# The first attention group's loads move into the last conv slot of the first pass, and the two query places change roles

## The chip, the cores and the metric

The kernel runs on one core of one Trainium2 chip, as one program. The metric is the device time of a run in microseconds (us). Five engines work side by side, each through its own list of instructions in order: TensorE (PE; its weight loads are PEld), VectorE (DVE), ScalarE (ACT), GpSimd (POOL) and SyncE (SP). SP computes nothing here: it issues nearly all DMAs, and its own waits are shown under the name SPq.

## The reference, cut to what matters

One layer of a hybrid encoder runs over 2048 prompt frames and 32 frames of a running stream, with 1024 channels. The input projection gives eight parts of 512 columns; four feed a conv branch and four an attention branch.

```python
xn = rmsnorm(x, norm_in)
h, bg, cg, zc, q, k, v, za = project_in(xn, w_in)        # xn @ w_in, split
yc = bg * short_conv(cg * h, conv_w, S) * jax.nn.silu(zc)
ya = band_attention(qc, k_band, v_band, rel, valid, rel_bias) * jax.nn.silu(za)
x = x + merge_out(yc, ya, norm_conv, norm_att, w_out)    # rmsnorm of each, then @ w_out
x = per_layer_embed(x, p, ple_norm, w_ple_gate, w_ple_proj)
y = rmsnorm(x, final_norm)
```

The band attention has 8 heads of 64 channels. A chunk of 64 frames attends to itself and to the 8 chunks before it. The 32 frames of the running stream attend to 512 cached keys and to themselves. Besides y, the newest keys, values and conv rows are returned.

## The kernel before

**Precision.** Every operand of a product is kept as a high and a low part in fp32r, and each product is three matmuls (high by high, high by low, low by high).

**On-chip memory.** One tile `GR` of 43,008 columns holds all matmul operands, at offsets written by hand. In the first part it holds the transposed input in five chunks of frames (`CHUNKS`; `Xh`, `Xl`) at columns 0 to 33,280. Chunk 0 (256 frames) lies at 0 to 4,096 and chunk 1 (384 frames) at 4,096 to 10,240. Two weight places `WS` follow, and from 41,472 (`O_SP`) 1,536 spare columns. Attention reuses the columns of chunks 0 and 1: keys `K` at 0 and 1,536, values `V` at 3,072, two places for transposed probabilities at 6,144 and 7,680, and the first of two query places at 9,216; the second query place and the two gate places `Z` lie in the spare columns.

**Stages.** (1) Projections of k, q, v and the attention gate, slot by slot; the results go to DRAM as `kd`, `qs`, `vd` and `zd`. (2) The conv branch: 8 slots `u`, each with two blocks of 128 weight columns, in `conv()`. The slots are passed three times: pass one over chunks 0 and 1 (`u` = 0 to 7), pass two over chunks 2 and 3 (8 to 15), pass three over chunk 4 (16 to 23). Pass one also stores the split weights in DRAM (`store_wc`, line 1054), and passes two and three read them back, 2 MB for a slot (`load_wc`, line 1060). (3) Beside passes two and three runs attention: `dense()` yields after every three conv matmuls, and the loop at the end hands out pieces of the generator `attention()` by the share of conv work done, from 3% (`FIRST`) on. (4) The output projection and the embedding, tile by tile.

**One conv slot.** For each chunk and block, 24 matmuls (line 1085) fill one PSUM bank. A slot of kind "B" then multiplies into `T2` (line 1102, DVE), applies the gate (line 1105 ACT, 1106 DVE), multiplies again (line 1107, POOL) and stores `T2` to `yd` (line 1108, SP). There is one `T2`: the next chunk's line 1102 needs that store to have landed. `conv()` yields 16 times for a chunk, the last time after the chunk's store.

**Attention.** There are 36 groups (4 head pairs by 9 spans of frames), and a step for each head. `load_kq(g)` loads a group's keys (line 447) and queries (line 454) for two heads in six DMAs of 128 KB; `load_vz(g)` loads its values (line 463, 256 KB) and gate (line 467, 128 KB). Queries of group g lie in `Q[g % 2]`. `emit_s(n, a)` (line 546) multiplies queries by keys on PE for one half of step n's frames; maximum, exponential, scaling, transposes (lines 618, 628) and the product with the values (lines 662, 664) follow.

**Order of SP.** SP issues in program order, and what it waits for holds up all behind it. At the end of pass one it issues, in this order: at `u` = 6 the weights of slot 8, four loads of the score bias (lines 474, 482) and the store of slot 7's weights (line 1054); in slot 7 the two stores of `T2`; then slot 9's weights; then the loads of attention groups 0 and 1. POOL masks the bias (lines 491, 492) before it comes to slot 7's line 1107.

```python
O_Q = [9216, O_SP]
    for u in range(8):
        s = NP1 + u
        store_wc(s)
        for i, _ in enumerate(conv(u, psm)):
            if i == KT:
                split_w(s + 1)
                load_w(s + 2)
        if u >= 6:
            load_wc(u + 2)
```

The functions that the change touches follow.

Of the kernel before, what the change touches and what calls it, by code (L numbers as in the profile page):

```python
# [26 lines left out]
KT = 8  # L27
# [12 lines left out]
O_SP = O_WS[1] + 4096  # L40
# [5 lines left out]
O_K = [0, 1536]  # L46
O_V = 3072
O_PT = [6144, 7680]
O_Q = [9216, O_SP]
O_Z = [O_SP + 1024, O_SP + 1280]  # L50

O_WO = XO[2]
# [11 lines left out]
def hybrid_encoder_kernel(  # L64
# [43 lines left out]
    def R(off, *shape):  # L108
        n = 1
        for s in shape:  # L110
            n *= s
        v = GR[:, off:off + n]
        return v if len(shape) == 1 else v.rearrange("p (a b) -> p a b", a=shape[0])
# [52 lines left out]
    def cols(kind, i):  # L166
        return DC * "hBCzqkva".index(kind) + 128 * i
# [8 lines left out]
    def load_w(s):  # L176
        if s >= NS:
            return
        (k0, i0), (k1, i1) = slots[s]
        if k0 == k1:  # L180
            c = cols(k0, i0)
            sp.dma_start(RAW, win[:, c:c + 256].rearrange("(k p) n -> p k n", p=128))
        else:
            for j, (kk, ii) in enumerate(slots[s]):
                c = cols(kk, ii)
                sp.dma_start(RAW[:, :, j * 128:(j + 1) * 128],
                             win[:, c:c + 128].rearrange("(k p) n -> p k n", p=128))

    def split_w(s, ks_=range(KT)):
        if s >= NS:  # L190
            return
        wh, wl = WS[s % 2]
        for k in ks_:
            act.activation(wh[:, k], RAW[:, k], AF.Copy, scale=cT[:, k:k + 1])  # L194
            dve.scalar_tensor_tensor(wl[:, k], RAW[:, k], cT[:, k:k + 1],  # L195
                                     wh[:, k].bitcast(F32), ALU.mult, ALU.subtract)
# [225 lines left out]
    K = [R(o, RING * 128) for o in O_K]  # L422
    Q = [[[R(o + 512 * h + 256 * b, 256) for b in range(2)] for h in range(2)] for o in O_Q]
    V = R(O_V, RING, 256)
# [13 lines left out]
    def load_kq(g):  # L438

        if g >= len(groups):  # L440
            return
        p, m = groups[g]
        t0, kn, qn = (256 * m, 256, 256) if m < 8 else (T, KW + S, S)
        k0 = t0 % (RING * 128)
        for h in range(2):
            rows = slice((2 * p + h) * HD, (2 * p + h + 1) * HD)
            sp.dma_start(K[h][:, k0:k0 + kn].bitcast(F32),
                         kd[:, rows, t0:t0 + kn].rearrange("b c t -> c b t"))
            for b in range(2):
                q = Q[g % 2][h][b]  # L450
                if m == 8:
                    pool.memset(q[:, 0:2 * S].bitcast(F32), 0.0)
                    q = q[:, h * S:(h + 1) * S]
                sp.dma_start(q[:, 0:qn].bitcast(F32),
                             qs[b, rows, t0:t0 + qn].unsqueeze(1).to_broadcast([HD, 2, qn]))

    def load_vz(g):
        if g >= len(groups):
            return
        p, m = groups[g]  # L460
        m0, m1 = (2 * m, 2 * m + 2) if m < 8 else (16, NKT)
        v0 = m0 % RING
        sp.dma_start(
            V[:, v0:v0 + m1 - m0, :].bitcast(F32),
            vd[m0 * 128:m1 * 128, 2 * p:2 * p + 2].rearrange("(m t) h a d -> t m (h a d)", t=128))
        t0, qn = 256 * m, 256 if m < 8 else S
        sp.dma_start(Z[g % 2][:, 0:qn], zd[p * 128:(p + 1) * 128, t0:t0 + qn])

    def load_bias(p):
        if p >= 4:  # L470
            return
        for h in range(2):
            base = ext2[2 * p + h:2 * p + h + 1]
            sp.dma_start(BIAS[p, h], bass.AP(tensor=base.tensor, offset=base.offset + 127,
                                             ap=[[767, 128], [1, 640]]))

    def load_bias8(p):
        if p >= 4:
            return
        for h in range(2):  # L480
            base = ext2[2 * p + h:2 * p + h + 1]
            sp.dma_start(BIAS8[h * S:(h + 1) * S],
                         bass.AP(tensor=base.tensor, offset=base.offset + 127,
                                 ap=[[767, S], [1, KW + S]]))

    def mask_bias(p):
        if p >= 4:
            return
        for h in range(2):
            t = BIAS[p, h]  # L490
            pool.memset(t[0:64, 576:640], BIG)
            pool.memset(t[64:128, 0:64], BIG)
# [530 lines left out]
    for s in range(2, NP1):  # L1023
        kind = slots[s][0][0]
        for c, (t0, n) in enumerate(CHUNKS):
# [11 lines left out]
            elif kind == "a":  # L1037
                for j, ps in enumerate((p0, p1)):
                    i = slots[s][j][1]
# [12 lines left out]
    def store_wc(s):  # L1052
        for b, w in enumerate(WS[s % 2]):
            sp.dma_start(wc[s - NP1, b], w.bitcast(F32).rearrange("p k n -> p (k n)"))

    def load_wc(u):
        if u >= 3 * 8:
            return
        for b, w in enumerate(WS[u % 2]):
            sp.dma_start(w.bitcast(F32).rearrange("p k n -> p (k n)"), wc[u % 8, b])  # L1060
# [63 lines left out]
# [4 lines that stand above are left out]
            if i == KT:  # L1128
                split_w(s + 1)
                load_w(s + 2)  # L1130
        if u >= 6:
            load_wc(u + 2)
        if u == 6:
            load_bias(0)
            load_bias8(0)
            mask_bias(0)

    load_kq(0)
    load_vz(0)
    load_kq(1)  # L1140
    banks = Ring([6, 7])

# [74 lines left out]
```

## Time and profile before

| What | Value |
|---|---|
| median of three runs | 1465.99 us (1465.03 to 1468.26) |
| profiled execution: its own time | 1465.2 us |
| profiled execution: its span, first to last instruction | 1463.2 us |
| busy, PE / PEld | 1426.2 us (97%) / 1269.9 us (87%) |
| busy, DVE / ACT / POOL | 609.4 us (42%) / 543.5 us (37%) / 314.0 us (21%) |
| mean granted TensorE clock | 0.992 of full speed |
| DMA | 249.10 MB, mean 170 GB/s |

Times inside the profile are us from the start of its span. The own time has 2.0 us more than the span, which lie around it. An engine's busy time is an average over stages with different limits; what one stage is worth is read from the waits of that stage.

### The profile page before, as it was taken

How to read it: one execution, taken by the hardware profiler on the slowest of the kernel's cores; microseconds unless marked ns; L12 is line 12 of the kernel's file. 1: busy time of each engine (PE TensorE's matmuls, PEld its weight loads, DVE VectorE, ACT ScalarE, POOL GpSimd, SP SyncE). 2: the span in 40 equal slices, each digit the busy share in tenths (PEclk: the TensorE clock that was granted, in tenths of full speed). 3: DMA queues.
4: the chain of work that ended last, by engine and by line, in shares of the span. 5: the costliest groups of instructions: out<-in, count | busy, mean ns of one | idle time of the engine just before them, and what ended most of it. 6: DMA issues, size and time to landing. Idle time of an engine off the chain costs nothing.

```text
span 1463.2 us, 22734 instructions
## 1 busy us (share of the span) xinstructions
PE 1426.2 (97%) x8362; PEld 1269.9 (87%) x8362; DVE 609.4 (42%) x1346; ACT 543.5 (37%) x1182; POOL 314.0 (21%) x438
## 2 busy tenths in 40 slices
PE   8999999999999979999999999998999999999997
PEld 8889989999899968888888888997788888888786
DVE  6323233330044326656555566653424333242333
ACT  7434233341233125544544544552122232232323
POOL 3310000000000013323332232331223232233322
PEclk9999999999999999999999999999999999999999
DMA  6536898884277555453555347666932212121100
GB/s 222 196 109 198 294 314 312 292 286 149 79 249 260 213 183 180 159 163 122 170 174 195 126 148 270 251 231 232 363 102 69 72 48 93 48 80 40 60 25 33
DMA packets 176391, 249.10 MB, mean 170 GB/s; under 512 B 19564, under 2 KB 124816, under 8 KB 170136
## 3 DMA queue, kind: packets, MB, share of 16 engines
q1 hardware_dynamic: 169712, 235.83, 47.6%
q10 hardware_dynamic: 6568, 11.82, 2.5%
q8 instruction: 66, 1.08, 0.3%
q14 instruction: 45, 0.37, 0.1%
HBM read 158.23 MB, written 92.50 MB: 171 GB/s over the span
## 4 chain that ended last, share of the span: by engine, by line
PE 86%; DMA 5%; DVE 3%; issue 2%; ACT 2%; SPq 1%; POOL 1%; POOLq 0%; DVEq 0%; ACTq 0%
PE PS L1085 20%; PE PS L279 17%; PE PS L280 16%; PE PS L281 16%; PE PS L546 5%; PE PS L664 3%; PE PS L618 3%; DMA GR<-wd 2%; PE PS L662 1%; PE PS L871 1%; DMA GR<-qs 1%; PE PS L829 1%; PE PS L268 1%; DMA GF<-ext 1%; DVE GF L1099 1%
## 5 line engine op out<-in xcount | busy, mean ns | idle before, releaser
L279 PE MATMUL PS<-GR 128*128 128x512 f32 (+3 forms) x1336 | 476.2, 356 | 2.9 <-DVE GF L1120 1.8
L280 PE MATMUL PS<-GR 128*128 128x512 f32 (+3 forms) x1336 | 471.9, 353 | 1.1 <-DVE GR L271 0.6
L281 PE MATMUL PS<-GR 128*128 128x512 f32 (+3 forms) x1336 | 471.9, 353 | 0.5 <-DVE GR L812 0.5
L1085 PE MATMUL PS<-GR 128*128 128x512 f32 (+3 forms) x1920 | 432.1, 361 | 0.6 <-DMA GR<-wc 0.6
L1085 PEld LDWEIGHTS PS<-GR 128*128 128x128 f32 x1920 | 310.8, 191 | 16.8 <-DMA GR<-wc 0.9
L279 PEld LDWEIGHTS PS<-GR 128*128 128x128 f32 x1336 | 253.2, 190 | 34.2 <-DVE GF L1120 2.1
L281 PEld LDWEIGHTS PS<-GR 128*128 128x128 f32 x1336 | 253.1, 189 | 31.6 <-DVE GR L812 1.0
L280 PEld LDWEIGHTS PS<-GR 128*128 128x128 f32 x1336 | 253.4, 190 | 30.9 <-DMA GR<-wd 1.1
L578 POOL TENSOR_SCALAR GF<-GF,SM 128x640 f32<-128x640 f32 (+3 forms) x132 | 98.5, 746 | 265.7 <-DVE SM L572 195.8
L593 DVE TENSOR_TENSOR GR<-PS,GR 128x256 fp32r<-128x256 f32 (+2 forms) x184 | 103.2, 562 | 98.9 <-ACT GR L592 98.7
L592 ACT ACTIVATE GR<-PS 128x256 fp32r<-128x256 f32 (+2 forms) x184 | 89.8, 489 | 78.4 <-PE PS L618 76.7
L1107 POOL TENSOR_TENSOR GF<-GF 128x512 f32<-128x512 f32 (+3 forms) x20 | 22.4, 1122 | 409.1 <-DVE GF L1106 408.4
L566 ACT ACTIVATE GF<-GF,SM 128x640 f32<-128x640 f32 (+3 forms) x132 | 99.9, 757 | 22.7 <-DVE SM L558 21.4
L558 DVE CUSTOM_DVE_ANT_0 GF<-PS,GF 128x640 f32<-128x640 f32 (+3 forms) x132 | 96.2, 729 | 24.7 <-PE PS L546 20.8
L546 PE MATMUL PS<-GR 128*128 128x320 f32 (+6 forms) x512 | 94.9, 307 | 11.7 <-DMA GR<-qs 7.4
L546 PEld LDWEIGHTS PS<-GR 128*128 128x128 f32 x512 | 81.4, 190 | 20.9 <-issue 7.7
L910 DVE TENSOR_TENSOR GF<-PS,GF 128x512 f32<-128x512 f32 (+2 forms) x35 | 23.6, 675 | 176.3 <-ACT GF L909 176.3
L909 ACT ACTIVATE GF<-PS,SM 128x512 f32<-128x512 f32 (+2 forms) x35 | 23.6, 675 | 163.9 <-PE PS L281 82.7
L664 PE MATMUL PS<-GR 128*128 128x256 f32 x448 | 78.0, 289 | 3.0 <-DVE GR L593 3.0
L195 DVE SCALAR_TENSOR_TENSOR GR<-GF,cT,GR 128x256 fp32r<-128x256 f32 x112 | 45.8, 480 | 73.9 <-ACT GR L194 73.9
L912 POOL TENSOR_TENSOR GF<-GF 128x512 f32<-128x512 f32 (+1 forms) x32 | 41.1, 1285 | 159.7 <-DVE GF L910 141.5
L671 ACT ACTIVATE GF<-PS 64x256 f32<-64x256 f32 (+1 forms) x72 | 26.0, 360 | 130.7 <-PE PS L664 124.2
(139 smaller groups left out, 1344.4 us busy)
## 6 DMA issues: line engine op xcount, KB each, us to landing
GR<-wc SPq DMA_DIRECT2D x32, 1024.0 KB, 7.3
GR<-wd SPq DMA_DIRECT2D x72, 256.0 KB, 6.8
GF<-in_x_prompt_dram SPq DMA_DIRECT2D x32, 512.0 KB, 7.6
wc<-GR SPq DMA_DIRECT2D x16, 1024.0 KB, 7.6
GR<-qs SPq DMA_DIRECT2D x128, 128.0 KB, 3.2
wd<-GF SPq DMA_DIRECT2D x50, 256.0 KB, 6.1
GF<-in_w_in_dram SPq DMA_DIRECT2D x20, 512.0 KB, 6.0
vd<-GF SPq DMA_DIRECT2D x40, 256.0 KB, 5.1
```

The costliest lines, as they stand in the source:

```text
L195: dve.scalar_tensor_tensor(wl[:, k], RAW[:, k], cT[:, k:k + 1], wh[:, k].bitcast(F32), ALU.mult, ALU.subtract)
L279: pe.matmul(out, wh(k), xh(k), start=(k == ks_[0]), stop=False)
L280: pe.matmul(out, wh(k), xl(k), start=False, stop=False)
L281: pe.matmul(out, wl(k), xh(k), start=False, stop=(k == ks_[-1]))
L546: pe.matmul(ps[:, e, c:c + n_], q[h][b][:, qa], K[h][:, r:r + n_], start=(b == 0 and c == 0), stop=(b == 1), skip_group_check=True)
L558: dve.tensor_tensor_reduce(pr.rearrange("p (b c) -> p b c", b=nb), ps, br.rearrange("p (b c) -> p b c", b=nb), 1.0, 3e38, ALU.add, ALU.min ...
L566: act.activation(pr, pr, AF.Exp, bias=mx[rows], scale=-1.0, accum_out=sm[rows])
L578: pool.tensor_scalar(pr, pr, rs[rows], 1.0, ALU.mult, ALU.mult)
L592: act.activation(dst_of(hi), src, AF.Copy)
L593: dve.tensor_tensor(dst_of(lo), src, dst_of(hi).bitcast(F32), ALU.subtract)
L664: pe.matmul(PS[:, PS_AV, 0:256], v(k), t[:, slot_of[k], :], start=(i == 0), stop=(i == len(both) - 1))
L1085: pe.matmul(ps, a[:, k, js], b[c][:, k, :], start=(k == i == 0), stop=(k == KT - 1 and i == 2))
```

## The change

`load_kq(0)` and `load_vz(0)` are called inside slot 7, after the yield that closes chunk 0 (`i == 2 * KT - 1`, which is 15), and no longer after the loop. The query place of even groups, group 0 among them, becomes the one in the spare columns, and that of odd groups the one at 9,216, inside chunk 1.

```diff
-O_Q = [9216, O_SP]
+O_Q = [O_SP, 9216]
...
             if i == KT:
                 split_w(s + 1)
                 load_w(s + 2)
+            if u == 7 and i == 2 * KT - 1:
+
+                load_kq(0)
+                load_vz(0)
         if u >= 6:
             load_wc(u + 2)
...
-    load_kq(0)
-    load_vz(0)
     load_kq(1)
     banks = Ring([6, 7])
```

SP, at the end of pass one, before (`wc` are stored weights, `yd` the conv results; the first kd to the first zd is group 0, what follows is group 1):

```order
L1054 DMA wc<-GR 128x2048 x2
L1108 DMA yd<-GF 128x256
L1108 DMA yd<-GF 128x384
L1060 DMA GR<-wc 128x2048 x2
L447 DMA GR<-kd 128x1x256
L454 DMA GR<-qs 128x1x256 x2
L447 DMA GR<-kd 128x1x256
L454 DMA GR<-qs 128x1x256 x2
L463 DMA GR<-vd 128x2x256
L467 DMA GR<-zd 128x256
L447 DMA GR<-kd 128x1x256
L454 DMA GR<-qs 128x1x256 x2
```

The same place in the changed kernel, with the semaphores that each issue waits for (DMAHW0 to DMAHW7 are eight that successive DMAs of SP take in turn):

```order
L1108 DMA yd<-GF 128x256 [waits DMAHW0_49,Pool_49]
L447 DMA GR<-kd 128x1x256 [waits DMAHW1_49,PE_49]
L454 DMA GR<-qs 128x1x256 [waits DMAHW2_49]
L454 DMA GR<-qs 128x1x256 [waits DMAHW3_49]
L447 DMA GR<-kd 128x1x256 [waits DMAHW4_49,PE_49]
L454 DMA GR<-qs 128x1x256 [waits DMAHW5_49]
L454 DMA GR<-qs 128x1x256 [waits DMAHW6_49]
L463 DMA GR<-vd 128x2x256 [waits DMAHW7_49]
L467 DMA GR<-zd 128x256 [waits DMAHW0_49]
L1108 DMA yd<-GF 128x384 [waits DMAHW1_49,Pool_49]
L1060 DMA GR<-wc 128x2048 [waits DMAHW2_49,PE_49]
L1060 DMA GR<-wc 128x2048 [waits DMAHW3_49,PE_49]
```

The eight loads of group 0 have moved ahead of two entries, the store of chunk 1's result and slot 9's weights; group 1's loads stay behind the weights. Each issue waits for the DMA eight places ahead of it.

PE, after slot 7, in the first part of slot 8, where attention's first matmuls (line 546) stand; - is before, + the change:

```order
 L1085 MATMUL PS<-GR 128x512 x30
-L546 MATMUL PS<-GR 128x128 [waits DMAHW5_49,DMAHW4_49,DVE_49]
-L546 MATMUL PS<-GR 128x128 [waits DMAHW6_49]
+L546 MATMUL PS<-GR 128x128 [waits DMAHW2_49,DMAHW1_49,DVE_49]
+L546 MATMUL PS<-GR 128x128 [waits DMAHW3_49]
 L1085 MATMUL PS<-GR 128x512 x9
 L546 MATMUL PS<-GR 128x256 [waits DVE_49]
 L546 MATMUL PS<-GR 128x256
 L1085 MATMUL PS<-GR 128x512 x6
```

No PE instruction moved; the same two matmuls wait for other semaphores, those of the keys (one) and of the two query loads of group 0's first head.

## Rows read from the trace of the kernel before

**Rows 1.** The page: span, chain that ended last, query loads (median us to landing).

```profile
span 1463.2 us, 22734 instructions
...
PE 86%; DMA 5%; DVE 3%; issue 2%; ACT 2%; SPq 1%; POOL 1%; POOLq 0%; DVEq 0%; ACTq 0%
...
GR<-qs SPq DMA_DIRECT2D x128, 128.0 KB, 3.2
```

**Rows 2.** PE's waits, whole span: waiter, releaser, total us, times, longest.

```profile
PE PS L546 <- DMA GR<-qs: 7.4, 1, 7.4
```

**Rows 3.** PE's timeline from 513: start, us, line, shape, [idle before <-releaser].

```profile
512.76 7.86 PE L1085 MATMUL PS<-GR 128*128 128x384 f32 x34
527.97 0.75 PE L546 MATMUL PS<-GR 128*128 128x128 f32 x2 [7.35 <-DMA GR<-qs]
528.52 3.89 PE L1085 MATMUL PS<-GR 128*128 128x512 f32 x9
...
538.12 0.52 PE L546 MATMUL PS<-GR 128*128 128x384 f32 x2
```

**Rows 4.** SP's timeline from 498: start, us until the last of them was issued.

```profile
502.07 1.75 SPq L1054 DMA_DIRECT2D wc<-GR  x2
511.95 7.01 SPq L1108 DMA_DIRECT2D yd<-GF  x2
519.07 0.87 SPq L1060 DMA_DIRECT2D GR<-wc  x2
519.99 0.60 SPq L447 DMA_DIRECT2D GR<-kd  x1
520.64 1.46 SPq L454 DMA_DIRECT2D GR<-qs  x2
...
527.11 0.33 SPq L467 DMA_DIRECT2D GR<-zd  x1
```

**Rows 5.** The chain of waits, 498 to 540: start, us, what.

```profile
499.73 10.14 DMA GF<-ext
...
511.95 4.38 DMA yd<-GF
...
517.61 1.01 POOL GF L1107
...
520.64 7.20 DMA GR<-qs
...
528.72 3.69 PE PS L1085 x9
...
534.02 0.17 PE PS L546 x2
534.19 1.42 PE PS L1085 x6
```

**Rows 6.** Windows of 1 us, PE: stretch, length, busy (count), granted clock, DMA share, GB/s.

```profile
514.00:515.00 1.00, 1.00 (x6) 1.00 0.25 92
...
517.00:518.00 1.00, 1.00 (x6) 1.00 0.00 0
...
526.00:527.00 1.00, 0.00 (x0) 0.50 0.94 336
...
532.00:533.00 1.00, 1.00 (x7) 1.00 0.51 143
```

**Rows 7.** ACT's timeline from 500: line 1105 after chunks 0 and 1 of slot 7.

```profile
504.87 0.39 ACT L1105 ACTIVATE GF<-PS 128x256 f32<-128x256 f32 x1 [9.03 <-PE PS L1085]
...
513.19 0.49 ACT L1105 ACTIVATE GF<-PS 128x384 f32<-128x384 f32 x1 [7.44 <-PE PS L1085]
```

**Rows 8.** Line 1054's DMAs from 498, issue to landing.

```profile
DMA to landing us min/median/max: 11.5/11.5/11.5
```

**Rows 9.** Windows of 5 us, all engines; the last two columns are DMA share and GB/s.

```profile
500.00:505.00 5.00, 5.00 (x43) 5.00 (x43) 0.99 (x3) 0.13 (x1) 0.00 (x0) 1.00 0.89 365
505.00:510.00 5.00, 5.00 (x31) 5.00 (x30) 1.66 (x3) 0.76 (x2) 0.08 (x1) 1.00 0.99 310
```

## The prediction

> **What bounds the kernel now.** Read the page first: the chain that ended last is 86% PE [rows 1], so the time is PE's work plus what PE waits for. The list of PE's waits comes next: the longest single wait of the whole span is 7.4 us, once, at line 546, for a query load [rows 2]. PE's own timeline shows the place: it runs conv matmuls without a gap from 512.76 to 520.62 (512.76 + 7.86), then stands until 527.97, when the first two matmuls of attention group 0 begin [rows 3]. The gap is 7.35 us.
>
> Why were the queries late? SP's timeline answers. SP issued chunk 0's store of slot 7 at 511.95 and then had nothing it could issue until chunk 1's store, because that store waits for POOL (line 1107, 517.61 to 518.62 [rows 5]); the two issues make one row that is 7.01 us long [rows 4]. Only then came slot 9's weights (2 MB, from 519.07), and behind them group 0's keys at 519.99 and queries at 520.64 [rows 4]. That query load took 7.20 us to land [rows 5], where the median of all 128 query loads is 3.2 us [rows 1]: it stood behind the 2 MB. Meanwhile, before 519, the DMA engines had fallen idle: busy share 0.25 in 514 to 515, 0.00 in 517 to 518 [rows 6].
>
> **The change, part by part.** Nothing is added or removed: the same eight DMAs of group 0 (1.15 MB: seven of 128 KB, one of 256) are issued after chunk 0's store and no longer behind the weights; no compute engine's order moves.
>
> *Where the loads go.* In the new order SP reaches them at about 512.3 (511.95 and one issue of some 0.3 us). A key load and its two query loads took from 519.99 to 522.10 to issue (520.64 + 1.46 [rows 4]), so the first head's three are out by 514.4 and the second's by 516.5; the values and the gate, at some 0.33 us as the gate's row has it [rows 4], would follow by 517.2. What can hold them: the keys overwrite chunk 0, whose last matmul PE had ended before ACT read its result at 504.87 [rows 7]; that is past. Group 0's queries go to spare columns, which nothing uses then. Each issue waits for the DMA eight places ahead: the sixth for the first half of the stored weights (issued at 502.07, landing after 11.5 us, so at 513.6 [rows 4, 8]), the seventh for the second half (issued by 503.82, so landed by 515.3), the eighth for chunk 0's store, which landed at 516.33 (511.95 + 4.38 [rows 5]). So all eight are issued by about 517.3, before POOL lets chunk 1's store go at 518.62. The first head's three, out by 514.4, land by about 517.6 with the median of 3.2 us, 3 us before PE comes to them at 520.62. If they were late the stall would come back by as much; with 3 us in hand I count it as gone: **7.35 us**.
>
> *The clock.* In the gap the granted clock fell: 0.50 in 526 to 527, that is 1.2 of 2.4 GHz, and it was back at 1.00 in 532 to 533 [rows 6]. The work done in between was slow: 0.75 us for two matmuls and 3.69 us for the nine conv matmuls behind them, 4.44 together [rows 3, 5]. At full clock two such matmuls take 0.17 us and six of line 1085 take 1.42, so nine take 2.13 [rows 5]; 2.30 together. Without the gap PE stays busy and this goes too: **2.14 us**. The two terms make 9.49.
>
> *What is late next.* Group 1's loads take the place in the queue that group 0's had: still behind slot 9's weights, a key and two queries at the same times. Group 0's second matmul, which needs the second query, began at about 528.55 (527.97 + 0.75 = 528.72, less one matmul at half clock, 0.17 [rows 3, 5]). PE came to group 1's first matmul at 538.12 [rows 3]; 9.49 earlier is 528.63, and the second follows some 0.1 later, at 528.73. The margin is 0.2 us. It shrinks if chunk 0's store lands later because loads now follow it: that store frees `T2`, then DVE, POOL, chunk 1's store, the weights and group 1 follow one another, each later by the same amount. No row shows this store with loads behind it. From below the delay is 0. From above the nearest row is the bias load, which was issued ahead of the stored weights and landed at 509.87 (499.73 + 10.14 [rows 5]). By 510 the engines had moved 3.38 MB (5 us at 365 GB/s and 5 at 310 [rows 9]), while slot 8's weights and the four bias loads make 2.89 MB (two of 1,024 KB, two of 320, two of 68, by the shapes). So about 0.5 MB that was issued later went through first: 1.4 us at 365 GB/s. A delay of 0 to 1.4 us leaves a wait of 0 to 1.2. I take half the delay, 0.7, since at most 0.77 MB follow here and not 2: a new wait of **0.5 us**.
>
> The Trainium skill has a rule on this, in "DMA: Bandwidth & Descriptors", section "Queues, rings and completion order": each DMA engine takes its descriptors in ring order, and the completion count lands after every earlier write of that engine. By it, loads behind the store would not come ahead of it, and the sum would be 9.5; by the row it is 8.3 to 9.5. The row decides, and it speaks for some overtaking.
>
> *The swapped places.* Odd groups' queries now lie in chunk 1, whose last matmuls were done when ACT read their result at 513.19 [rows 7]; group 1's queries are issued after 519.07. Cost nothing; the cover is 6 us.
>
> *Does the gain stay?* All later loads are issued on PE's progress or wait for buffers that PE frees, so what follows shifts as one piece.
>
> **Sum.** 7.35 + 2.14 - 0.5 = 9.0 us. Against the profiled execution, 1465.2 (span 1463.2 and 2.0 around it), that gives 1456.2. The median of the runs shown, 1465.99, stands 0.8 above that execution; from it the forecast is **1457.0**.
>
> **Rivals.**
> - *The wait moves to group 1* (10%). If slot 9's weights and group 1's loads come 3 us later than before, PE waits 2.8 us for them: gain 6.7, 1459.3; with 5 us late 4.8 us, gain 4.7, 1461.3. For it: the margin of 0.2 us, and the query row: 7.20 us behind the weights, 3.2 otherwise [rows 1, 5]. Against: SP is free at about 517.3, before chunk 1's store can go. The skill's rule above is this mechanism in general: group 1's counts cannot land before the weights ahead of them, with which the 7.20 us agrees.
> - *The loads are not early* (4%). If the first three are held on SP, or land as slowly as behind the weights and more, they miss 520.62 and the old wait returns in part or whole: 1460 to 1466. For it: at 512.3 the stored weights are still moving (their second half is issued by 503.82 and lands by 515.3). Against: by 514 to 515 the engines' share was down to 0.25 [rows 6], and the first three wait on SP only for slot 8's weights and the bias loads, which POOL's masking needed before chunk 0's store could go.
> - *Slower: SP is held* (4%). The sixth to eighth load wait on SP for the stored weights and for chunk 0's store. If those land late, SP comes late to chunk 1's store, the weights and group 1. A delay d beyond 518.62 costs PE d less 0.2, and once the wait is as long as the old one, another 2.14 for the clock; that equals what is saved at d = 7.6, and beyond it the change loses. With 12 us: 11.8 + 2.14 - 9.49 = 4.4 slower, 1470.4. Against: DMA engines idle in 517 to 518 [rows 6], so d would have to come from landings that are some 9 us later than in this trace.
>
> **Numbers.** A measurement of this kernel tells about 0.2%, 2.9 us, from no change. The forecast has 82%, the rivals 10, 4 and 4. Faster by more than that takes in the forecast and most of the first rival, 0.91; no change the rest of it and most of the second, 0.05; slower the third, 0.04. The range goes down to 1454.8: no new wait (0.5 more), runs that lie 1.0 below their median as the lowest before did, and 0.7 for the difference between profile and median. Up it goes to 1461.3, which holds the first rival to 5 us late.
>
> **What would show it.** Right: in the changed profile SP issues the keys of group 0 right behind chunk 0's store, at about 512.3; line 546 has no wait for a query load there; the granted clock stays 1.00 from 514 to 535; PE comes to group 1 at about 528.6 and waits at most 1 us there; the span is near 1454.2. Wrong: a wait of some us at group 1's line 546; DVE's line 1102 of chunk 1 well after 517; or the gap gone and the span no shorter, which would mean that something after 540 is not tied to PE.

## The result, and the profile after

| | before | change |
|---|---|---|
| median of six runs each | 1465.51 us (1462.56 to 1468.26) | 1454.28 us (1452.22 to 1458.57) |
| ratio, 95% interval | | 0.9929 (0.9907 to 0.995) |
| profiled execution: own time / span | 1465.2 / 1463.2 us | 1455.54 / 1453.5 us |
| mean granted clock | 0.992 | 0.995 |

The change makes the kernel 0.7% faster. The ratio on the median that the forecast started from, 1465.99, gives 1455.6; forecast were 1457.0 and 1454.8 to 1461.3. The raw median of the six runs lies 0.5 us below that range; the runs of before taken beside them were lower too.

The page of the changed kernel, and PE's waits over the whole span:

```profile
span 1453.5 us, 22734 instructions
...
PE 86%; DMA 6%; DVE 3%; ACT 2%; issue 2%; SPq 1%; POOL 1%; POOLq 0%; DVEq 0%; ACTq 0%
```

```profile
PE PS L546 <- DVE SM L558: 4.3, 4, 1.7
...
PE PS L546 <- DMA GR<-qs: 0.7, 1, 0.7
```

The 7.4 us of [rows 2] are 0.7 now. SP's timeline (start, us until the last was issued) answers to [rows 4]:

```profile
512.25 0.32 SPq L1108 DMA_DIRECT2D yd<-GF  x1
512.67 0.60 SPq L447 DMA_DIRECT2D GR<-kd  x1
513.32 1.24 SPq L454 DMA_DIRECT2D GR<-qs  x2
...
517.20 0.47 SPq L467 DMA_DIRECT2D GR<-zd  x1
518.99 0.32 SPq L1108 DMA_DIRECT2D yd<-GF  x1
519.40 0.86 SPq L1060 DMA_DIRECT2D GR<-wc  x2
520.32 0.53 SPq L447 DMA_DIRECT2D GR<-kd  x1
520.89 1.28 SPq L454 DMA_DIRECT2D GR<-qs  x2
...
528.92 0.33 SPq L467 DMA_DIRECT2D GR<-zd  x1
```

Group 0's eight loads stand between the two stores, and the last was issued by 517.67, before chunk 1's store was free to go. All that is ahead of them came 0.30 us later than in the execution of before (512.25 against 511.95), so 0.30 is to be taken off when times of the two are compared here. PE's timeline, against [rows 3]:

```profile
520.76 0.33 PE L546 MATMUL PS<-GR 128*128 128x128 f32 x2
520.93 2.27 PE L1085 MATMUL PS<-GR 128*128 128x512 f32 x9
...
524.65 0.33 PE L546 MATMUL PS<-GR 128*128 128x128 f32 x2
...
529.77 0.71 PE L546 MATMUL PS<-GR 128*128 128x384 f32 x2 [0.69 <-DMA GR<-qs]
```

Group 0 begins without a wait, and the nine conv matmuls behind it take 2.27 us and not 3.89. The only wait for a query that is left is 0.69 us, at group 1. The next head's first two matmuls, at 524.65 here, stood in the kernel before at:

```profile
533.86 0.33 PE L546 MATMUL PS<-GR 128*128 128x128 f32 x2
```

The chain and the windows of 1 us show two numbers that matter for the cause of the wait at group 1:

```profile
512.25 4.42 DMA yd<-GF
...
520.89 8.74 DMA GR<-qs
```

```profile
518.00:519.00 1.00, 1.00 (x6) 1.00 0.98 303
...
526.00:527.00 1.00, 1.00 (x7) 1.00 0.94 330
```

Chunk 0's store landed after 4.42 us, as in [rows 5] with 4.38; group 1's first query took 8.74 us, where group 0's had taken 7.20 in that place. The clock stays at 1.00 in the stretch that showed 0.50 in [rows 6].

**Where the gain is.** Group 1's first matmul came at 538.12 [rows 3] and comes at 529.77: 8.35 us earlier, 8.65 with the 0.30. How far the lead holds is seen at line 650, which each head pair runs once; PE's timelines, before first:

```profile
646.79 1.39 PE L650 MATMUL PS<-GR 128*128 128x256 f32 x10
764.31 1.34 PE L650 MATMUL PS<-GR 128*128 128x256 f32 x10
880.17 1.39 PE L650 MATMUL PS<-GR 128*128 128x256 f32 x10
```

```profile
638.63 1.39 PE L650 MATMUL PS<-GR 128*128 128x256 f32 x10
754.54 1.33 PE L650 MATMUL PS<-GR 128*128 128x256 f32 x10
870.28 1.39 PE L650 MATMUL PS<-GR 128*128 128x256 f32 x10
```

The lead is 8.16 us at the first, 9.77 at the second, 9.89 at the third, and 9.7 at the end of the span. The 1.6 us between the first and the second are not tied to the change. Both kernels wait 1.97 us for DVE there (line 662), and behind that wait the clock fell in the one execution and not in the other, as windows of 2 us show, before first:

```profile
662.00:664.00 2.00, 2.00 (x7) 0.50 0.32 107
```

```profile
652.00:654.00 2.00, 1.66 (x9) 1.00 0.28 85
654.00:656.00 2.00, 2.00 (x13) 1.00 0.40 124
```

In the experiments below it can be the other way round: behind the same wait the clock fell to 0.50 in an execution that has the change (the fetch moved out) and stayed at 1.00 in one that has not (the weights loaded twice).

### The profile page after: what moved, and what is told of

The parts are those of the page before. It is cut to its first block, busy times and chain, and to the rows that moved or that the text cites. A ratio compares the mean times of both kernels' runs of the same rounds, so it can differ in the third digit from the quotient of the medians.

```text
span 1453.5 us, 22734 instructions
## 1 busy us (share of the span) xinstructions
PE 1422.6 (98%) x8362; PEld 1267.2 (87%) x8362; DVE 609.7 (42%) x1346; ACT 543.3 (37%) x1182; POOL 314.0 (22%) x438
## 4 chain that ended last, share of the span: by engine, by line
PE 86%; DMA 6%; DVE 3%; ACT 2%; issue 2%; SPq 1%; POOL 1%; POOLq 0%; DVEq 0%; ACTq 0%
PE PS L1085 19%; PE PS L279 17%; PE PS L280 17%; PE PS L281 17%; PE PS L546 5%; PE PS L664 3%; PE PS L618 3%; DMA GR<-wd 2%; PE PS L662 1%; DMA GR<-qs 1%; PE PS L871 1%; PE PS L829 1%; PE PS L268 1%; DMA GF<-ext 1%; DVE GF L1099 1%
```

## Experiments

### The swap alone

The kernel before, with the two query places exchanged and the loads left where they were.

```diff
-O_Q = [9216, O_SP]
+O_Q = [O_SP, 9216]
```

> The kernel before with only the two query places swapped; the loads stay behind slot 9's weights. My theory (the gain is the vanished wait and the clock it cost): nothing moves, ratio to the kernel before 1.000 within 0.002, line 546 waits some 7.4 us for group 0's queries and the granted clock falls to 0.50 behind it. Rival (the place of the queries matters by itself): a part of the 10 us already shows here.

Measured: ratio 0.9998 (0.9989 to 1.0007) in 11 runs, and the wait is there again in PE's timeline:

```profile
527.79 0.72 PE L546 MATMUL PS<-GR 128*128 128x128 f32 x2 [7.34 <-DMA GR<-qs]
528.31 4.11 PE L1085 MATMUL PS<-GR 128*128 128x512 f32 x9
```

The places cost and bring nothing by themselves. The swap only makes the early issue possible, since the place at 9,216 is still read in slot 7.

### Ahead of the weights, but after the slot

The kernel before; group 0's loads go out when slot 7 is over, ahead of slot 9's weights.

```diff
+        if u == 7:
+            load_kq(0)
+            load_vz(0)
         if u >= 6:
             load_wc(u + 2)
...
-    load_kq(0)
-    load_vz(0)
     load_kq(1)
```

> The kernel before with group 0's eight loads issued after slot 7, but ahead of slot 9's weights; no swap. My theory: the first head's three loads go out at 519.0 to 521.2 and land some 2.9 us later, near 524; line 546 waits 3 to 3.5 us instead of 7.35, and the granted clock, which fell 4.8 us after the wait began, does not fall, so the 2.14 us go too. The weights go out some 5 us later, so group 1's queries land near 533 and PE waits another 1.5 to 2 us for them. Sum: 4 to 5 us faster than before, about half of the change's gain. Rival (all of it is the queue behind the weights, the place inside the slot adds nothing): the whole gain of the change, 9 to 10 us.

Measured: ratio 0.9981 (0.9972 to 0.999), so 2.8 us of the change's 10. PE's timeline and the windows of 1 us:

```profile
523.68 0.30 PE L546 MATMUL PS<-GR 128*128 128x128 f32 x1 [1.95 <-DMA GR<-qs]
524.13 0.33 PE L546 MATMUL PS<-GR 128*128 128x128 f32 x1 [0.16 <-DMA GR<-qs]
524.30 2.31 PE L1085 MATMUL PS<-GR 128*128 128x512 f32 x9
...
535.14 0.73 PE L546 MATMUL PS<-GR 128*128 128x384 f32 x2 [2.64 <-DMA GR<-qs]
```

```profile
537.00:538.00 1.00, 1.00 (x4) 0.50 0.73 224
```

The first wait shrinks to 2.11 us, and the clock is spared behind it, as the theory has it: the nine matmuls take 2.31 us. But the second wait, at group 1, is 2.64 us and not 1.5 to 2, and behind it the clock fell, which the theory did not count; so the gain was smaller than the 4 to 5 us expected. That the place inside the slot is worth most of the gain holds, and the rival (the queue order is all) falls.

### Group 1 ahead of the weights as well

The change, with `load_kq(1)` moved ahead of slot 9's weights.

```diff
+        if u == 7:
+            load_kq(1)
         if u >= 6:
             load_wc(u + 2)
...
-    load_kq(1)
     banks = Ring([6, 7])
```

> The change, and group 1's keys and queries also ahead of slot 9's weights (after slot 7). My theory: group 1's first query lands by 524, the wait of 0.69 us at line 546 goes, slot 9's weights land some 4 us later than in the change, long before slot 9; span 0.7 us shorter than the change's, to be seen in the profile and too small for the clock of whole runs. Rival (the later weights become the wait): line 1085 waits for them near 545.

Measured: no wait of PE for a load between 500 and 560, span 1452.4 against 1453.5, line 1085 waits for no weights there. The ratio to before is 0.9926 (0.9913 to 0.994) with a median of 1454.47: not to be told from the change itself.

### Values and gate late

The change, with group 0's values and gate behind group 1's keys and queries.

```diff
                 load_kq(0)
-                load_vz(0)
...
     load_kq(1)
+    load_vz(0)
```

> The change, with group 0's values and gate issued behind group 1's keys and queries instead of in slot 7. My theory of the new wait (group 0's 1.15 MB were still moving when the weights went out, so group 1's query landed after 8.74 us and not after 7.20): with 0.38 MB less ahead, group 1's query lands after some 7.3 us and line 546 waits 0 to 0.2 us; the values now land near 531 and line 664 waits for them, 1 to 2 us. Rival (chunk 0's store is held up by the loads behind it, the cause that the prediction named): group 1's query stays at 8.7 us.

Measured: ratio 0.9949 (0.9934 to 0.9965). PE's timeline and, for the moment before the weights go out at 519.29, a window of 1 us:

```profile
529.51 0.73 PE L546 MATMUL PS<-GR 128*128 128x384 f32 x2 [0.56 <-DMA GR<-qs]
531.73 0.35 PE L664 MATMUL PS<-GR 128*128 128x256 f32 x1 [1.50 <-DMA GR<-vd]
```

```profile
518.00:519.00 1.00, 1.00 (x6) 1.00 0.03 9
```

The wait at line 664 is the one expected. But the wait for group 1's query stays, 0.56 us, though the DMA engines were all but idle (share 0.03 and not 0.98) just before the weights were issued, and the first query still took 8.58 us to land. So group 0's loads, left over in the engines, are not why group 1's are late: that theory falls. The rival of this run, the store held up by the loads behind it, had already fallen to the 4.42 us above. A third cause was needed.

### The instruction fetch moved out of the weights

One packet differs. In the view of DMA queues, a 16 KB packet of a queue called "instruction" falls among slot 9's weights in the change (window 525 to 526) and behind them in the kernel before (531 to 532), change first:

```profile
q8 instruction: 1, 0.02, 6.2%
```

```profile
q8 instruction: 1, 0.02, 7.0%
```

The last column is the share of 16 engines' time, so 6.2% of 1 us is one engine for 1.0 us. The whole span has 66 such packets; PE's 8,362 matmuls and 8,362 weight loads, divided by 66, are 253 instructions for each. The Trainium skill says in "Runtime: NRT & Kernel Launch", section "Instruction fetch mechanics", that an engine's instructions are refilled in blocks of 16 KiB, 256 instructions, through a DMA queue of its own; the counts here agree with that. So a longer list of PE instructions ahead should move the packet:

```diff
-    for _ in range(14):
+    for _ in range(38):
         pe.matmul(PS[:, 4, 0:128], ident, ident, start=True, stop=True)
```

> The change with 24 more warm-up matmuls (48 in the trace) at the kernel's start: nothing else moves but the place at which PE's instruction list crosses from one fetched block to the next. All times lie some 5 to 8 us later; what counts is the place itself. Theory (PE's 16 KB instruction fetch, one packet of 1.0 us on one DMA engine, fell among slot 9's weights and made that engine, and all that waits for it, late): the fetch now falls before the weights go out, the second half of the weights lands 7.5 us after its issue and not after 8.9, group 1's query 7.2 us after its issue and not 8.7, and line 546 waits for no query. Rival (loads land later because PE reads on-chip memory while they write, and it stands still in the kernel before): 8.9 and 8.7 us again, and a wait of 0.7 us.

Measured (this run and the three that follow were timed once each): the packet lies in 518 to 519, ahead of the weights, which go out at 523.42. PE's timeline and SP's:

```profile
524.83 0.33 PE L546 MATMUL PS<-GR 128*128 128x128 f32 x2
...
532.99 0.52 PE L546 MATMUL PS<-GR 128*128 128x384 f32 x2
```

```profile
523.42 0.88 SPq L1060 DMA_DIRECT2D GR<-wc  x2
...
531.61 0.33 SPq L467 DMA_DIRECT2D GR<-zd  x1
```

No wait at group 1. The second query load of the group behind the weights lands 7.1 us after its issue; it took 6.8 in the kernel before, 6.9 with the swap alone, 7.3 in the run that follows, all with the packet elsewhere, and 8.4 in the change. With the values late, where the packet lay among the weights too (525 to 526), it took 8.3, with its last step 1.3 us behind the others: that is why that wait stayed. SP's gate load of group 1, which waits for the weights' second half, came 8.19 us after the weights' first issue here (531.61 - 523.42) and 9.52 in the change (528.92 - 519.40). PE works through the weights' landing in this run as in the change, so the rival (PE's reads slow the loads) falls.

How the load is late points to one held engine. The trace counts a load's landing in sixteen steps of its semaphore. For the second half of slot 9's weights the last two steps came at 526.96 and 527.10 in the kernel before, at 531.44 and 531.59 in this run, but at 527.19 and 528.90 in the change: fifteen were in time, and one came 1.71 us behind them. In this run the late step begins where the packet lies now, near 518.6: the stored weights, landing before it, end with steps at 518.64 and 518.92, and chunk 0's store behind them with 519.02 and 520.68.

### The fetch moved into the weights of the kernel before

```diff
-    for _ in range(14):
+    for _ in range(21):
```

> The kernel before with 7 more warm-up matmuls (14 in the trace), so that PE's instruction fetch, which came at 531.0, falls just ahead of the 7.35 us wait, among slot 9's weights. Times lie 1 to 3 us later. Theory of the fetch: the weights' second half and group 0's query land up to 1.4 us later, line 546 waits 8.2 to 8.8 us. Rival (PE's standing still is what makes loads fast): the wait stays 7.3 to 7.4 us. If the fetch misses the weights, this run tells nothing.

Measured: the packet came in 531 to 532, again after the weights had landed; the weights went out at 520.08, and the gate load that waits for their second half at 528.50. The fetch missed them, and the run tells nothing about the wait, as foreseen for that case. The wait, 6.04 us, is shorter because PE came later to it (at 523.34 and not 520.62).

### The weights loaded twice

```diff
+    load_wc(9)
     load_kq(0)
     load_vz(0)
```

> The kernel before with slot 9's weights loaded twice ahead of group 0's loads, which about doubles the one wait. My theory: line 546 waits 14 to 15 us; the granted clock falls as before, some 5 us after the wait began, and comes back about 4.5 us after PE works again, so the clock costs the same 2.1 us and not twice that; span 7 to 7.5 us longer than before's. Rival (the clock's price grows with the wait): over 4 us lost at the low clock.

Measured: span 1471.3, and 1465.1 for the kernel before, run beside it: 6.2 us longer and not 7 to 7.5, one execution against one. PE's timeline, and windows of 1 us:

```profile
533.69 0.77 PE L546 MATMUL PS<-GR 128*128 128x128 f32 x2 [13.71 <-DMA GR<-qs]
534.26 4.15 PE L1085 MATMUL PS<-GR 128*128 128x512 f32 x9
...
540.49 0.33 PE L546 MATMUL PS<-GR 128*128 128x128 f32 x2
```

```profile
523.00:524.00 1.00, 0.00 (x0) 0.50 1.03 434
...
540.00:541.00 1.00, 1.00 (x7) 1.00 0.73 224
```

From group 0's first matmul to the next head's first (the two rows of two matmuls) this takes 6.80 us, in the kernel before 5.89 (533.86 - 527.97) and in the change 3.89 (524.65 - 520.76). The clock's price is 2.9 us behind a wait of 13.71, and 2.0 behind one of 7.35. It is more than the 2.1 expected and not twice as much; the rival's 4 us falls. That fits a price that is paid after the wait, until the clock is back, and not during it.

### The bias loaded early

The change, with the bias loads and masks at the end of slot 4.

```diff
-        if u == 6:
+        if u == 4:
             load_bias(0)
             load_bias8(0)
             mask_bias(0)
```

> The change, with the bias loads and masks at the end of slot 4 and not of slot 6. My theory: POOL's line 1107 of slot 7 no longer stands behind the masks (bias landed at 509.87 in the kernel before); chunk 0's store goes out at about 506.5 and not 512, lands near 511 to 514 behind the stored weights, chunk 1's store follows at 515 to 516 and not 519, slot 9's weights behind it, and group 1's query is there before PE: no wait at line 546 for a query, span some 0.7 us below the change's, which is less than runs differ. Rival: the stored weights hold chunk 0's store as long as the masks did, and nothing moves.

Measured: span 1454.1. POOL's and SP's timelines:

```profile
504.81 1.16 POOL L1107 TENSOR_TENSOR GF<-GF 128x256 f32<-128x256 f32 x1 [18.57 <-DVE GF L1106]
```

```profile
506.00 0.32 SPq L1108 DMA_DIRECT2D yd<-GF  x1
...
515.12 0.32 SPq L1108 DMA_DIRECT2D yd<-GF  x1
515.54 0.88 SPq L1060 DMA_DIRECT2D GR<-wc  x2
```

POOL now waits for DVE and no longer for the bias, both stores and the weights go out 4 to 6 us earlier, and no wait for a query is left at line 546. So the bias and its masks were what held slot 7's tail, and the reading of that chain was right. The instruction packet came in 523 to 524, just behind the weights, and the second query took 8.6 us, but it had gone out 4 us earlier and was there before PE. The span is no shorter than the change's: 0.7 us is less than what executions differ by.

## Why the prediction was right, point by point

- **The stall, 7.35 us: right.** PE's wait at group 0 is gone. The loads went out where forecast (keys at 512.67, all eight by 517.67, against 512.3 and 517.3). Line 447 waited for nothing that delayed it.
- **The clock, 2.14 us: right, 0.14 too large.** From group 0's first matmul to the next head's first PE took 5.89 us before (533.86 - 527.97) and takes 3.89 (524.65 - 520.76): 2.00 us. The step reckoned 2.30 us at full clock for the first eleven of these matmuls; they take 2.44 (523.20 - 520.76).
- **The new wait, 0.5 us: near in size by luck, wrong in cause.** 0.69 us came. The step said that chunk 0's store would land later for the loads behind it, by up to 1.4 us; it landed after 4.42 us and 4.38 before, so this delay was nothing. The rule of the Trainium skill that was weighed there ("DMA: Bandwidth & Descriptors", section "Queues, rings and completion order": descriptors are taken in ring order, and a count lands after the earlier writes of its engine) agrees with this row. What made group 1 late was PE's instruction fetch, which met the weights because PE now reached it while they moved, and that was in no rival. The run with the fetch moved out shows it. The bound of 1.4 us was misread as well: of the bias load's sixteen steps in the kernel before, the fifteenth came at 507.78 and the last at 509.87, with an instruction packet at 502.0 among the transfers ahead of it. In the run with the packet ahead of slot 8's weights (500.5 against 501.60; seven more warm-up matmuls) they came at 510.10 and 510.15. So this row showed the same fetch, and not later loads that overtake.
- **The sum.** 7.35 + 2.14 - 0.5 = 9.0 was forecast for this place; 8.65 us were found at group 1, and 7.35 + 2.00 - 0.69 makes 8.66. The two profiled executions differ by 9.7 us; the rest of that is the 1.6 us of clock further on, which one execution lost and the other did not, less the 0.3 and small differences. The ratio's interval, 0.9907 to 0.995, stands for a gain of 7.3 to 13.6 us, and cannot tell 9 from 10.
- **The rivals.** The wait did move to group 1 in part, by 0.69 us of the first rival's 2.8 or more. SP was not held, and the loads were early.
- **"What follows shifts as one piece": right.** The lead was 8.16 us a hundred microseconds later; what it gained by the second of the three places is the clock's.

## What to carry to other kernels

When an engine waits for a load that stands behind a large one, look at what the issuing engine did before: here it stood for over 6 us waiting to issue a store, and the DMA engines fell idle meanwhile. Loads whose place is free belong into that time, and it was worth exchanging two buffers so that the place is free; issuing them only ahead of the large load, when the wait of the issuing engine is over, kept some 3 of 10 us. The stall cost more than its length, since PE worked at the lower clock (0.50) behind it: 2.0 us more for 7.35, 2.9 more for 13.71.

## What the hardware showed that was not expected

- **An instruction fetch delays data.** One 16 KB packet kept one DMA engine for 1.0 us, and the second query behind the weights landed 8.4 us after its issue with the packet among the weights, 8.3 with it there and the values late, and 6.8 to 7.3 in the four runs with the packet elsewhere. With the loads ahead of the weights but after the slot, where the packet (527 to 528) came as the weights began to move, it took 7.5. The Trainium skill ("Runtime: NRT & Kernel Launch", section "Instruction fetch mechanics") calls the cost of crossing such a block mostly hidden; for PE it was (busy 1.00 in 525 to 526), but not for the loads, of whose sixteen steps one came 1.7 us late.
- **Clock falls after short waits come and go.** Behind the same wait of 1.97 us at line 662 the clock fell to 0.50 in the profiled execution of before and stayed at 1.00 in the change's, 1.6 us apart. The change's six runs go from a span of 1450.2 us at a mean granted clock of 0.997 to 1456.7 at 0.991. That all of this spread comes from such falls was not tested.
